# Even attention of a two-layer inference step: the value products of a head moved into one run, one head later, with TensorE held to the program's order

## Chip, cores and metric

The kernel runs on one core of one Trainium2 chip. The metric is the time of one execution on the device in microseconds, the median of the runs made; lower is better.

## What is computed

The reference is one step of a two-layer backbone on 128 prompt tokens and 512 sample tokens of width 1024. The even layer has two groups of eight attention heads: multi-head latent attention (MLA, query and key of 64 + 32 columns, values of 64) and grouped-query attention (GQA, 64 columns, two key/value heads). Prompt tokens attend to the prompt; sample tokens attend to 128 cached and 512 own keys. The odd layer, not touched here, has mLSTM and differential attention. Cut to the even layer:

```python
def attend(q, k, v):                       # scale = dk ** -0.5, blocks of 128 queries
    s = jnp.einsum('bqhgd,bthd->bhgqt', qi, k).astype(jnp.float32) * scale
    p = jax.nn.softmax(s, axis=-1).astype(v.dtype)
    return jnp.einsum('bhgqt,bthd->bqhgd', p, v)
...
o_a = attend(q_a, k_a, v_a).reshape(B, S, MLA_W) * jax.nn.silu(g_a)
o_b = attend(q_bg, kb_all, vb_all).reshape(B, S, GQA_W) * jax.nn.silu(g_b)
return jnp.concatenate([o_a, o_b], axis=-1) @ w_out, new
...
m = jax.nn.silu(cvec) @ w + b              # adaLN: shift, scale, gate of a layer
```

## The kernel before

The program is written with Tile: the text makes tiles and instructions, and a scheduler, which keeps a model of the time line, puts the instructions of each engine in an order; on the chip each engine then works in that order and waits on semaphores. Line numbers below are those of the kernel before; in the changed kernel, lines from the helper `ada_load` to the loop of `attention` stand 13 higher, lines behind that loop 23.

`even_attention` (TensorE's work from 222.8 to 402.2 us) runs 16 heads, 0 to 7 MLA and 8 to 15 GQA, over the 512 sample queries. A score tile (`head_scores`, `scores`, L596) is 128 queries by 640 keys, so a head has four of them, `i` = 0 to 3. It takes six matmuls of 320 keys for MLA (three passes over high and low parts) and four for GQA, into the PSUM tag `s2`, which has two buffers. `softexp` takes the maximum on VectorE (L603, `nm`), the exponentials and their sum on ScalarE (L606, `p` and `sm`), and the reciprocal on VectorE (L609, `rs`); GpSimd multiplies (L616). `p` has ten buffers.

For each of five key tiles `k` the four probability tiles of a head are transposed on TensorE into one PSUM tile (`head_T`, L623, tag `t1`, two buffers) and copied to SBUF as `pT` (L626 on VectorE for `k` = 2, L628 on ScalarE for the others; three buffers). `head_PV` (L634) multiplies the values of that key tile with `pT` into `o`: two matmuls in the text, which the trace shows as four, each 64 columns of the array wide. At the end of a head VectorE multiplies `o` into the gated output `og` (L710, two halves).

The loop of `attention` writes, for a head `h`, transposes of tile `k`, then the value product of tile `k - 1`, with the queries of head `h + 2` (`prep`, L764 for MLA, L749 for a pair of GQA heads), side work and score tiles in between; score tiles run up to ten ahead. The side work (`side`) is adaLN columns of the odd layer for heads 0 to 7 (`ada_cols`, L177, 32 columns of the array wide; then a ScalarE copy `adap`, two transposes L184, and small VectorE operations L186 to L195), and for heads 8 to 15 partial gate rows (`ada_gate_part`, L210), the loads and splits of the output projection's weights (`op_load`, L75 to L77) and the split of `og` into high and low parts (`op_split`, L841 and L842). The prompt's own attention goes as four `prompt_quad` pieces between the heads: scores `sp` in the tag `s2` (L647), transposes `t1p` (L660), value product `op` (L668).

PSUM has eight banks, all in use: two `s2` tiles of two banks, two `t1`, one `o`, one `pr` for queries and side work. The order between all of these is the scheduler's; in the trace of before TensorE goes from scores to transposes to value products and back many times in a head.

## Time and profile before

| | before |
|---|---|
| time, median of 3 runs | 910.01 us (910.0 to 910.73) |
| profiled execution, span from first to last instruction | 905.8 us |
| busy in the span: TensorE matmul | 852.9 us (94%) |
| VectorE, ScalarE, GpSimd | 541.2, 422.6, 396.6 us |
| even attention, 222.8 to 402.2: length, TensorE busy | 179.4, 173.66 us |
| same stage: VectorE, ScalarE, GpSimd busy | 124.35, 116.65, 103.61 us |

The profile is of one execution; the median of the runs lies 4.2 us above its span. PE is TensorE's matmuls, PEld its weight loads, DVE VectorE, ACT ScalarE, POOL GpSimd, SP the queue that issues most transfers. The chain that ended last, by the profile, is TensorE for 74% of the span and VectorE for 16%.

### The profile page before, as it was taken

The numbers are of one execution on the slowest core, as the hardware profiler recorded it, in microseconds if no ns is written. First come the engines' busy times: TensorE is split into PE (matmuls) and PEld (weight loads), VectorE is DVE, ScalarE is ACT, GpSimd is POOL, SyncE is SP. The second block draws the span as 40 slices with busy tenths as digits, with TensorE's granted clock in tenths as the row PEclk, the third lists the DMA queues.
The fourth block names the chain that finished last, engine by engine and source line by source line (L and its number), as shares of the span: only waits on it lengthen the run. The fifth ranks groups of instructions, "written<-read, shape, count | busy, mean of one in ns | idle before, by whom it ended". The sixth has DMA issues, their size and how long they took to land.

```text
span 905.8 us, 14374 instructions
## 1 busy us (share of the span) xinstructions
PE 852.9 (94%) x5418; PEld 707.2 (78%) x5418; DVE 541.2 (60%) x1125; ACT 422.6 (47%) x928; POOL 396.6 (44%) x302
## 2 busy tenths in 40 slices
PE   6999899979999999999999999999999899999997
PEld 2778788879776766668887889889989688778786
DVE  3773831993866877641386735077774736666765
ACT  5354523311655677752263324266554656443422
POOL 0144424751754646725535333422221946354930
PEclk9999999999999999999999999999999999999999
DMA  9821222220221222324412212222123122142503
GB/s 347 330 65 35 88 87 71 70 71 24 94 94 53 84 98 93 119 77 176 152 47 105 86 71 94 81 70 71 47 93 129 58 88 63 55 164 75 163 1 117
DMA packets 29641, 88.52 MB, mean 98 GB/s; under 512 B 3752, under 2 KB 6880, under 8 KB 29572
## 3 DMA queue, kind: packets, MB, share of 16 engines
q1 hardware_dynamic: 25904, 83.64, 26.4%
q10 hardware_dynamic: 3668, 3.96, 1.3%
q8 instruction: 43, 0.70, 0.3%
q14 instruction: 26, 0.21, 0.1%
HBM read 80.90 MB, written 6.68 MB: 97 GB/s over the span
## 4 chain that ended last, share of the span: by engine, by line
PE 74%; DVE 16%; issue 3%; ACT 3%; POOL 2%; DMA 1%; SPq 0%; POOLq 0%; ACTq 0%; DVEq 0%
PE acc L84 11%; PE acc L85 11%; PE acc L83 11%; PE s L596 7%; PE acc L1060 6%; PE o L634 5%; PE t L623 5%; PE acc L120 3%; PE o L1146 2%; PE pv L1460 2%; PE ada L177 1%; POOL wlo L77 1%; DVE nm L603 1%; PE gps L210 1%; PE acc L544 1%
## 5 line engine op out<-in xcount | busy, mean ns | idle before, releaser
L77 POOL TENSOR_TENSOR wlo<-raw,whi 128x1024 fp32r<-128x1024 f32 (+4 forms) x79 | 185.8, 2357 | 229.8 <-ACT whi L76 222.7
L85 PE MATMUL acc<-whi,Hl 128*128 128x512 f32 (+2 forms) x400 | 148.5, 373 | 1.6 <-DVE Hl L958 1.6
L84 PE MATMUL acc<-wlo,Hh 128*128 128x512 f32 (+2 forms) x400 | 149.2, 373 | 0.2 <-POOL wlo L77 0.2
L83 PE MATMUL acc<-whi,Hh 128*128 128x512 f32 (+2 forms) x400 | 138.9, 374 | 1.0 <-ACT qk L1064 1.0
L76 ACT CAST whi<-raw 128x1024 fp32r<-128x1024 f32 (+4 forms) x71 | 71.6, 1010 | 131.2 <-PE acc L85 80.5
L603 DVE TENSOR_REDUCE nm<-s 128x1 f32<-128x640 f32 (+1 forms) x104 | 80.9, 780 | 57.1 <-PE s L596 56.0
L616 POOL TENSOR_TENSOR p<-p,rs 128x640 f32<-128x640 f32 x64 | 79.7, 1256 | 64.2 <-DVE rs L609 62.6
L606 ACT ACTIVATE p<-s,nm 128x640 f32<-128x640 f32 (+1 forms) x104 | 79.4, 764 | 59.8 <-DVE nm L603 53.9
L85 PEld LDWEIGHTS acc<-whi,Hl 128*128 128x128 f32 x400 | 75.3, 188 | 14.7 <-DVE Hl L958 1.8
L83 PEld LDWEIGHTS acc<-whi,Hh 128*128 128x128 f32 x400 | 75.1, 188 | 14.0 <-ACT qk L1064 1.2
L84 PEld LDWEIGHTS acc<-wlo,Hh 128*128 128x128 f32 x400 | 75.4, 188 | 12.9 <-POOL wlo L77 0.6
L48 POOL TENSOR_TENSOR rs_r<-rs_h,mhalf 128x1 f32<-128x1 f32 (+4 forms) x39 | 35.6, 921 | 53.4 <-DVE rs_h L47 45.0
L623 PEld LDWEIGHTS t<-cst,p 128*128 128x128 f32 x320 | 34.6, 140 | 23.6 <-issue 22.1
L623 PE MATMUL t<-cst,p 128*128 128x128 f32 x320 | 51.3, 283 | 0.2 <-POOL p L616 0.2
L84 PE MATMUL acc<-wlo,oh 128*128 128x512 f32 (+1 forms) x124 | 48.1, 388 | 0.1
L85 PE MATMUL acc<-whi,ol 128*128 128x512 f32 (+1 forms) x124 | 47.8, 386 | 0.0
L83 PE MATMUL acc<-whi,oh 128*128 128x512 f32 (+1 forms) x124 | 46.7, 389 | 0.0
L628 ACT COPY pT<-t 128x512 f32<-128x512 f32 x64 | 37.1, 584 | 17.4 <-PE t L623 17.0
L120 PE MATMUL acc<-Hh,whi 128*128 128x320 f32 x128 | 31.3, 316 | 6.9 <-DVE og L129 6.9
L63 DVE TENSOR_REDUCE ssq<-sq 128x2 f32<-128x128 f32 (+3 forms) x19 | 11.5, 604 | 40.6 <-ACT sq L61 40.4
L885 ACT ACTIVATE junk<-xt 128x512 bf16<-128x512 f32 (+1 forms) x21 | 12.8, 610 | 49.0 <-DVE xt L883 37.7
L1060 PE MATMUL acc<-Hh,whi 128*128 128x320 f32 x128 | 32.5, 323 | 0.5 <-ACT v L1037 0.5
(380 smaller groups left out, 1983.2 us busy)
## 6 DMA issues: line engine op xcount, KB each, us to landing
adaw<-in_eada_ss_dram SPq DMA_DIRECT2D x16, 512.0 KB, 10.3
raw<-in_oada_ss_dram SPq DMA_DIRECT2D x16, 512.0 KB, 4.3
raw<-in_e_wG_dram SPq DMA_DIRECT2D x8, 512.0 KB, 3.3
raw<-in_eada_g_dram SPq DMA_DIRECT2D x8, 512.0 KB
raw<-in_e_wO_dram SPq DMA_DIRECT2D x8, 512.0 KB, 4.2
raw<-in_oada_g_dram SPq DMA_DIRECT2D x8, 512.0 KB, 3.5
raw<-in_o_wO_dram SPq DMA_DIRECT2D x8, 512.0 KB, 3.9
xT<-in_xT_dram SPq DMA_DIRECT2D x8, 320.0 KB, 5.8
```

The lines of the kernel that those rows point to most:

```text
L76: (cp or nc.scalar.copy)(hi[:, 0:m], raw[:, 0:m])
L77: nc.gpsimd.tensor_tensor(out=lo[:, 0:m], in0=raw[:, 0:m], in1=hi[:, 0:m], op=ALU.subtract)
L83: mm(out, lhsT=lh, rhs=rh, start=first, stop=False)
L84: mm(out, lhsT=lh, rhs=rl, start=False, stop=False)
L85: self.mark = mm(out, lhsT=ll, rhs=rh, start=False, stop=last)
L120: mm(acc[j][:, 0:320], lhsT=a[:, k], rhs=b[:, k, j * 320:j * 320 + 320], start=f, stop=l)
L596: self.mark = self.nc.tensor.matmul(out[:, j, 0:w], lhsT=q[0:rows, qcols], rhs=k[0:rows, a:a + w], start=i == 0, stop=i == len(passes) - 1)
L603: nc.vector.tensor_reduce(out=nm, in_=s, axis=AX.XY, op=ALU.max, negate=True)
L606: nc.scalar.activation(out=p[:, 0:n].rearrange("p (a b) -> p a b", a=s.shape[1]), in_=s, func=AF.Exp, bias=nm, accum_out=sm)
L616: self.nc.gpsimd.tensor_tensor(out=p, in0=p, in1=rs.to_broadcast([128, 640]), op=ALU.mult)
L623: self.nc.tensor.transpose(tp[:, i * 128:i * 128 + 128], p[i][:, k * 128:k * 128 + 128], self.ident)
L1060: nc.tensor.matmul(acc[j][:, 0:320], lhsT=a[:, k], rhs=b[:, k, j * 320:j * 320 + 320], start=f, stop=l)
```

## The change

Value products (`head_PV`) leave the loop over key tiles. A new inner function `values(h, pt)` issues all five of a head in one run and then the gating products; it is called in the next head, after that head's second transposition (`k` = 1), and once more at the end. `pT` therefore has seven buffers instead of three, and `p` eight instead of ten. The loop has five steps instead of six, the prompt stages come at `k` = 3 and 4 instead of 3 and 5, and the side work of heads 0 to 7 is one adaLN tile each, its second half (`rest`) one step later, where before head 0 had two and head 5 none. And a new context manager `pe_order` gives every TensorE instruction of the stage a dependency on the one before it in the text, so that the scheduler can no longer reorder TensorE there; the other engines' order is still the scheduler's.

```diff
+    @contextmanager
+    def pe_order(self):
+        ins = lambda: self.nc.cur_bb.bb.instructions
+        first = ins()[-1]
+        yield
+        now = list(ins())
+        at = next(k for k in reversed(range(len(now))) if now[k] is first) + 1
+        pe = [i for i in now[at:] if i.engine == self.mark.ins.engine]
+        for a, b in zip(pe, pe[1:]):
+            self.tc.add_manual_dep(b, a.name, mybir.DependencyInfo(mybir.DependencyClass.NoSync,
+                                                                   mybir.DependencyReason.DATA), reason="pe_order")
...
-        p, rs = self.softexp(T, s, 640, 10)
+        p, rs = self.softexp(T, s, 640, 8)
...
-        pT = T.tile([128, 512], F32, tag="pT", name="pT", bufs=3)
+        pT = T.tile([128, 512], F32, tag="pT", name="pT", bufs=7)
...
-        for h in range(nh):
+        def values(h, pt):
             o = ps.tile([128, 512], F32, tag="o", name="o", bufs=1)
-            pt = {}
-            p = [tiles.pop((h, i)) for i in range(4)]
-            for k in range(6):
-                if k < 5:
-                    pt[k] = self.head_T(T, ps, p, k)
-                if k:
-                    self.head_PV(o, V[h], cols[h], pt.pop(k - 1), k - 1)
-                if k == 0 and h + 2 < nh:
-                    prep(h + 2, P)
-                if k == 2:
-                    side(h)
-                if k in (3, 5):
-                    next(stages, None)
-                more_scores(4 * h + 5 + 1 + min(k, 3) + (1 if k >= 4 else 0))
+            for k in range(5):
+                self.head_PV(o, V[h], cols[h], pt[k], k)
             r = slice(64 * (h % 2), 64 * (h % 2) + 64)
             for j in range(2):
                 g = self.og[r, h // 2, 128 + 256 * j:384 + 256 * j]
                 nc.vector.tensor_tensor(out=g, in0=o[64 * j:64 * j + 64, 0:256], in1=g, op=ALU.mult)
+        last = None
+        for h in range(nh):
+            pt = []
+            p = [tiles.pop((h, i)) for i in range(4)]
+            for k in range(5):
+                pt.append(self.head_T(T, ps, p, k))
+                if k == 0 and h + 2 < nh:
+                    prep(h + 2, P)
+                if k == 1 and last:
+                    values(*last)
+                if k == 2:
+                    rest = side(h)
+                if k == 3 and rest:
+                    rest()
+                if k in (3, 4):
+                    next(stages, None)
+                more_scores(4 * h + 5 + 1 + min(k, 3) + (1 if k >= 4 else 0))
+            last = h, pt
+        values(*last)
...
             if h < 8:
-                for i in ((0, 1), (2,), (3,), (4,), (5,), (), (6,), (7,))[h]:
-                    self.ada_cols("o", i, ps, "pr", 1)
-                return
+                return self.ada_cols("o", h, ps, "pr", 1, split=True)
...
-        self.attention(T, ps, P, prep, [Va] * 8 + [Vb] * 8, [64 * h for h in range(8)] + [64 * (h // 4) for h in range(8)],
-                       side, quads)
+        with self.pe_order():
+            self.attention(T, ps, P, prep, [Va] * 8 + [Vb] * 8, [64 * h for h in range(8)] + [64 * (h // 4) for h in range(8)],
+                           side, quads)
```

The rest of the diff takes comments out. How the order moves shows at three places. In the rows, `s` is a score tile, `t` a transposition, `o` a value product (two matmuls in the program for each key tile, so a run of a head is x10), `gps` a gate product; the number behind a name tells tiles apart.

TensorE in a GQA head, before:

```order
L596 MATMUL s_3743<-Kb,q 128x320 x4
L634 MATMUL o<-pT,Vb 64x256 x2
L623 MATMUL t_3696<-cst,p 128x128 x4
L596 MATMUL s_3765<-Kb,q 128x320 x4
L634 MATMUL o<-pT,Vb 64x256 x2
L623 MATMUL t_3734<-cst,p 128x128 x4
L634 MATMUL o<-pT,Vb 64x256 x2
L623 MATMUL t_3756<-cst,p 128x128 x4
L596 MATMUL s_3810<-Kb,q 128x320 x4
```

and TensorE in a GQA head now, from the last step of one value run to the next:

```order
L609 MATMUL s_3680<-Kb,q 128x320 x4
L636 MATMUL t_3693<-cst,p 128x128 x4
L223 MATMUL gps<-raw,sc 32x128 x8
L609 MATMUL s_3716<-Kb,q 128x320 x4
L636 MATMUL t_3729<-cst,p 128x128 x4
L609 MATMUL s_3736<-Kb,q 128x320 x4
L636 MATMUL t_3749<-cst,p 128x128 x4
L609 MATMUL s_3756<-Kb,q 128x320 x4
L636 MATMUL t_3769<-cst,p 128x128 x4
L772 MATMUL qtp<-cst,qb 128x128 x4
L636 MATMUL t_3787<-cst,p 128x128 x4
L647 MATMUL o<-pT,Vb 64x256 x10
```

Where a value product stood between most transposes, there is now one run behind the second transposition of a head, and score tiles and transposes alternate. In the text of the sections that follow, V is such a run; T0 to T4 are the transposes of a head's five key tiles; s6 and s7 are the two score tiles behind V (here 3680 and 3716), which complete the next head, and s8 and s9 the two after them (3736 and 3756), the first of the head after that. T0 of the next head is here 3769.

TensorE in an MLA head with prompt scores (`sp`) now, from the score tile s7 on:

```order
L609 MATMUL s_2499<-Ka_1593,ql 128x320 x2
L636 MATMUL t_2514<-cst,p 128x128 x4
L197 MATMUL ada<-cst,adap 128x128 x2
L800 MATMUL qtp<-cst,qa 128x128 x4
L609 MATMUL s_2542<-Ka_1595,qh 128x320 x2
L609 MATMUL s_2542<-Ka_1596,qh 128x320 x2
L609 MATMUL s_2542<-Ka_1595,ql 128x320 x2
L636 MATMUL t_2557<-cst,p 128x128 x4
L660 MATMUL sp<-kp_1597,qp 128x128
L660 MATMUL sp<-kp_1598,qp 128x128
L660 MATMUL sp<-kp_1597,qp 128x128 x2
```

The prompt scores of a quad stand together between T4 and s9; before, the scheduler had put other score matmuls among them.

VectorE in head 8, where the first half of `og` is split, before:

```order
L710 TENSOR_TENSOR og<-o,og 64x256 x2
L842 TENSOR_TENSOR ol_3718<-og,oh_3717 128x512
L626 COPY pT<-t_3579 128x512
L609 RECIPROCAL rs<-sm 128x1
L603 TENSOR_REDUCE nm<-s_3648 128x1
L842 TENSOR_TENSOR ol_3845<-og,oh_3844 128x512
L842 TENSOR_TENSOR ol_3962<-og,oh_3961 128x512
L603 TENSOR_REDUCE nm<-s_3683 128x1
L842 TENSOR_TENSOR ol_4083<-og,oh_4082 128x512
L842 TENSOR_TENSOR ol_4206<-og,oh_4205 128x512
L609 RECIPROCAL rs<-sm 128x1
```

and now:

```order
L713 TENSOR_TENSOR og<-o,og 64x256 x2
L616 TENSOR_REDUCE nm<-s_3563 128x1
L864 TENSOR_TENSOR ol_3713<-og,oh_3712 128x512
L639 COPY pT<-t_3576 128x512
L864 TENSOR_TENSOR ol_3840<-og,oh_3839 128x512
L864 TENSOR_TENSOR ol_3957<-og,oh_3956 128x512
L616 TENSOR_REDUCE nm<-s_3599 128x1
L864 TENSOR_TENSOR ol_4078<-og,oh_4077 128x512
L864 TENSOR_TENSOR ol_4201<-og,oh_4200 128x512
L622 RECIPROCAL rs<-sm 128x1
```

The five subtractions stand among the maxima of the score tiles s6 and s7 (3563 and 3599) nearly as before; the reciprocal behind them is now that of s6.

## Rows read from the trace of the kernel before

**Rows 1.** Stretches: length, busy us (instructions) by engine, granted clock, DMA share, GB/s.
```profile
core 0: us, PE busy (x) PEld busy (x) DVE busy (x) ACT busy (x) POOL busy (x), PEclk, DMA share, GB/s
222.80:402.20 179.40, 173.66 (x1384) 118.82 (x1383) 124.35 (x261) 116.65 (x272) 103.61 (x80) 1.00 0.26 90
232.00:236.00 4.00, 2.89 (x27) 1.54 (x25) 3.23 (x6) 2.36 (x11) 3.92 (x5) 1.00 0.52 168
896.00:906.00 10.00, 3.06 (x26) 2.85 (x25) 3.73 (x11) 2.36 (x6) 1.10 (x2) 0.86 0.28 105
```

**Rows 2.** Timeline of TensorE: start us, busy us, line, output and inputs, count.
```profile
266.28 1.07 PE L177 MATMUL ada<-raw,sc 128*32 128x256 f32 x16
267.28 0.85 PE L596 MATMUL s<-Ka,qh 96*128 96x320 f32 x4
...
332.19 0.64 PE L210 MATMUL gps<-raw,sc 128*32 128x128 f32 x16
332.76 0.85 PE L596 MATMUL s<-Kb,q 128*128 128x320 f32 x4
...
357.92 0.66 PE L623 MATMUL t<-cst,p 128*128 128x128 f32 x4
358.50 0.65 PE L634 MATMUL o<-pT,Vb 128*64 128x256 f32 x4
359.09 0.66 PE L623 MATMUL t<-cst,p 128*128 128x128 f32 x4
...
363.45 0.83 PE L596 MATMUL s<-Kb,q 128*128 128x320 f32 x4
364.12 0.60 PE L623 MATMUL t<-cst,p 128*128 128x128 f32 x4
...
392.38 1.08 PE L634 MATMUL o<-pT,Vb 128*64 128x256 f32 x8
393.39 0.66 PE L623 MATMUL t<-cst,p 128*128 128x128 f32 x4
```

**Rows 3.** Timeline of score tiles through the engines (the last column: idle before).
```profile
234.07 1.30 POOL L616 TENSOR_TENSOR p<-p,rs 128x640 f32<-128x640 f32 x1
...
356.55 0.85 PE L596 MATMUL s<-Kb,q 128*128 128x320 f32 x4
357.44 0.82 DVE L603 TENSOR_REDUCE nm<-s 128x1 f32<-128x640 f32 x1 [0.67 <-PE s L596]
358.36 0.80 ACT L606 ACTIVATE p<-s,nm 128x640 f32<-128x640 f32 x1 [0.59 <-DVE rs L609]
359.35 0.16 DVE L609 RECIPROCAL rs<-sm 128x1 f32<-128x1 f32 x1 [1.01 <-ACT p L606]
359.55 2.47 POOL L616 TENSOR_TENSOR p<-p,rs 128x640 f32<-128x640 f32 x2
```

**Rows 4.** Groups of the stage: line, engine, operation, count, busy us, mean ns, idle before.
```profile
L710 DVE TENSOR_TENSOR og<-o,og 64x256 f32<-64x256 f32 x31 | 13.0, 418 | 8.8 <-PE o L634 8.4
L626 DVE COPY pT<-t 128x512 f32<-128x512 f32 x16 | 10.9, 684 | 0.7 <-PE t L623 0.4
L842 DVE TENSOR_TENSOR ol<-og,oh 128x512 fp32r<-128x512 f32 x5 | 6.3, 1292 | 0.0
L193 DVE TENSOR_SCALAR adat<-adar,cols 128x2 f32<-128x2 f32 x8 | 4.9, 614 | 0.0
L190 DVE TENSOR_SCALAR So<-adar,cols 128x2 f32<-128x2 f32 x8 | 3.5, 441 | 0.2
L760 DVE CAST Ka<-kn 64x640 fp32r<-64x640 f32 x6 | 3.1, 519 | 0.1
L315 DVE TENSOR_TENSOR qp<-qtp,qp 128x512 fp32r<-128x512 f32 x2 | 1.4, 692 | 2.1 <-ACT qp L314 2.1
L628 ACT COPY pT<-t 128x512 f32<-128x512 f32 x64 | 37.1, 584 | 17.4 <-PE t L623 17.0
L841 ACT CAST oh<-og 128x512 fp32r<-128x512 f32 x6 | 3.4, 626 | 0.0
```

More of the change, by code (lines that the diff above doesn't have):

```diff
@@ L1 @@
 import math
-from contextlib import ExitStack
+from contextlib import ExitStack, contextmanager
 import numpy as np
@@ L660, in prompt_quad @@
             nc.tensor.transpose(tp[:, j * 128:j * 128 + 128], p[:, j], self.ident)
-        pT = T.tile([128, 512], F32, tag="pT", name="pTp", bufs=3)
+        pT = T.tile([128, 512], F32, tag="pT", name="pTp", bufs=7)
         nc.vector.tensor_copy(pT, tp)
```

## Prediction, made before the changed kernel ran

> **What bounds the kernel now.** I read the stretch table first. The even attention fills 179.4 us of the 905.8 us span, from the first scores at 222.8 to the first product of the output projection at 402.2, and TensorE is busy for 173.66 of them: 5.7 us idle, with VectorE, ScalarE and GpSimd all far below it [rows 1]. So today TensorE sets the time of this stage, and whatever the stage gains or loses is passed on: the linear work behind it waits for its last product.
>
> Next I read TensorE's own timeline, start to start. Four transposes after a value product and before another take 0.58 us, four value matmuls between transposes 0.59 (358.50 to 359.09), but eight value matmuls 1.01 (392.38 to 393.39): four more cost 0.43, so about 0.15 us is paid each time TensorE goes from 128-column work (scores s, transposes t) to 64-column work (o) or back. Between s and t nothing of that kind shows: four score matmuls take 0.67 up to the transposes of 364.12, which is 4 times 0.147 and little else [rows 2]. The gate products (32 columns) pay the same price on both sides.
>
> Third, the chain of one score tile. A GQA tile whose scores start at 356.55 has its maximum at 357.44, its exponentials at 358.36, its sum's reciprocal at 359.35 and its GpSimd normalisation at 359.55; two of those take 2.47, so one is 1.25 and ends at 360.80 [rows 3]. From the start of the scores to the first moment at which a transpose can read the tile is 4.3 us with nothing in the way. For MLA heads (six score matmuls, not four) it is 4.6.
>
> **What is saved.** The order of before has 181 changes between 128-, 64- and 32-column work in this stage, that of after 69, with the same matmuls. 112 changes at 0.15 us are 16.8 us. If TensorE stayed as full as now, the stage would take 179.4 - 16.8 = 162.6 us. TensorE's own work becomes 173.7 - 16.8 = 156.9 us.
>
> The Trainium skill, "TensorEngine Tiling (Array Packing)", section Key Properties, says that changing the tiling mode drains TensorE; the 0.15 us is what that costs here, and by that rule alone the change could only win. It says nothing on what fills the time instead, which is the rest of this sum.
>
> **What is lost.** The new order is fixed, and it leaves TensorE little to do where before a value product stood ready. The last transpose of T0 (the first key tile of the next head) needs all four normalised tiles. The youngest of them, s7, is scored in the head before; between the two stand only T3, a score tile, T4 and a score tile. Value products no longer help: the whole run V comes behind T0 and T1. The tile's chain therefore closes a loop, V, s6, T2, s7, chain of s7, T0, T1, V, and its length, not TensorE's work, is a head's period. I walked the loop with the rows' durations and each engine's order of after, time 0 where V ends:
>
> GQA head with a gate product: s6 at 0, T2 0.66, gate 1.19 (0.57 [rows 2]), s7 1.76. VectorE first does two gating products (0.42 each [rows 4]), then the maximum of s6, the copy of T2 (0.68), and the maximum of s7 at 2.66. ScalarE has the copies of the gate product and of T3 (0.58) first, so s7's exponentials run 3.76 to 4.56, its sum to 4.75; normalisation 5.0 to 6.25. TensorE was ready for T0 at about 5.3 (s9 has to wait for s7's PSUM buffer, 4.65). T0's last transpose goes at 6.34; then T1, 0.5 to V, and V: 5 x 0.43 + 0.15 = 2.3. Period 9.3 us, 9.74 where a query transpose stands between. TensorE's work in it is 7.75: **1.55 us idle** in each of heads 9 to 13, 7.8 in all.
>
> MLA head with prompt transposes and prompt value product (2, 4, 6): s7 at 2.48 (adaLN product 1.0 [rows 2]), its maximum 3.66 to 4.48. On VectorE the key cast (0.52), the prompt copy (0.68) and two small adaLN operations (0.44, 0.61) stand ahead of s7's reciprocal, which comes at 7.0; T0's end at 8.57, work until V 11.2 in a period of 12.0: **0.8** each, 2.4. MLA head with prompt scores (1, 3, 5): these wait for the prompt query's low part (0.69 on VectorE, behind the adaLN operations) until 7.65, and since they take a PSUM buffer of the score pair, s9 waits for the exponentials of s8 until 9.4. Work 11.7, period 14.1: **2.4** each, 7.2. Head 7: 2.6.
>
> Head 8 carries the splitting of the output projection's first half: five casts on ScalarE (0.63 each) and five subtractions on VectorE (1.29 each [rows 4]) come between its score tiles; the maximum of s7 has three of the five ahead of it and s6's reciprocal all. Before has nearly the same VectorE order and TensorE lost one wait of 1.6 us to it, with value products to fill the rest; the bounds are 1.6 and 6.3, and I take 6.3 plus the usual 1.55, **7.9**, since the run V has gone already. Head 14 has two gate products and a weight split ahead of its last tile: **3.7**; the tail of head 15: 0.6.
>
> Start. Until the fourth tile of head 0 is normalised, TensorE has four score tiles, a query transpose, the prompt scores and three transposes: 5.6 us of work. In before that tile is done at 235.4 [rows 3]; TensorE meanwhile did a score tile and an adaLN product of later, and it was busy for 2.89 of 4 us from 232 [rows 1]. From 222.8 to 234.9 that leaves 6.4 idle; head 0, without any V, leaves 3.1 (score tiles two apart wait for each other's PSUM). Together **9.5**.
>
> Sum of idle: 9.5 + 2.4 + 7.2 + 2.6 + 7.8 + 7.9 + 3.7 + 0.6 = 41.7 us. The stage: 156.9 + 41.7 = 198.6, against 179.4: **19.2 us more**. The profiled execution ends 19.2 later, at a span of 925.0; the median of the runs stands 4.2 us above the span, and 910.0 + 19.2 = 929.2.
>
> At nothing I cost: two probability buffers fewer (the exponentials of s8 now wait for T4, which by the walk is done before ScalarE gets to them); the adaLN products spread evenly over heads 0 to 7; the gate row, which comes 20 us nearer to the end of the stage (its way through DRAM is covered by the first half of the output projection, some 14 us of products that need no gate); one weight load moved ahead of the gate row on SP. If that cover failed it would cost a few us at the projection's first evacuation.
>
> **The rivals.** (a) TensorE stays as full as before and keeps the 16.8 us: 893. For it: 97% busy today. Against it: the period of the loop is above the work in every kind of head. (b) The other side: the same loop with half the idle, because the orders of VectorE and ScalarE collide less than in my walk. The sign turns where the idle of the stage falls under 179.4 - 156.9 = 22.5 us, about 1.4 us a head. Without any collisions a GQA head's period is 8.9 (V 2.3, T0 to V 0.6, s7 at 1.76 + 4.3), so 1.1 idle, an MLA head's is near its work; with the start that is 15 to 28 us idle, and 902 to 916, middle 908. Against it: in before the chains from scores to a normalised tile are often longer than 4.3, the casts and subtractions of head 8 are real, and VectorE's rows stand in a fixed order. (c) More than I count, over 55 us idle: 943 and above; each collision delays the next head too.
>
> (d) A lower clock. The granted clock is 1.00 over the stage, also from 232 to 236; at the end of the kernel, with TensorE busy for 3.06 of 10 us, it is 0.86 [rows 1]. A fall to the lower level in head 8's stall would double up to one head's 7.75 us of work, a part of it idle anyway: about 935. The longest stall I expect is some 6 us in pieces, so it is unlikely.
>
> The Trainium skill, "TensorE: Matmul & The Clock Gate", section Why this matters for your kernels, warns of idle gaps between bursts of matmuls in mid-kernel, after which the clock drops to half; by that rule, (d) is what to look for.
>
> **How the numbers follow.** Forecast (idle 30 to 55 us, 918 to 943): 0.72; (b) 0.14; (a), with all that ends under 902: 0.05; (c) 0.05; (d) 0.04. A measurement of this kernel can tell about 0.2%, 1.8 us, from no change. Faster by more: (a) and two thirds of (b), 0.14. Within 0.2%: 0.05. Slower: 0.81. For 8 in 10 the range leaves out (a) and the lower part of (b), and most of (c): 904 to 945.
>
> **What would show it.** Right: in the stage's table TensorE's busy time near 157 of 199 us; idle just before the transposes, released by GpSimd's normalisation, 1 to 2 us in nearly every head, and a stall of several us at head 8 released by VectorE; value runs of 2.3 us; GQA periods of 9.3 to 9.7. Wrong: transposes that follow scores with no wait, or value runs that take 2.9 (no saving). The linear stages should keep their lengths. Should normalised tiles be ready within 2.6 us of GQA scores, the loop is no bound and (a) holds.

## The result, and the profile after

The changed kernel takes 933.12 us, the median of four runs (930.64 to 935.39), against 910.0 us for the kernel before: a ratio of 1.0256, 95% interval [1.0221, 1.0291]. The profiled execution is the one of 935.39 us, with a span of 933.6.

The stretch table of the changed kernel comes first (length, then busy us and instructions of TensorE, its weight loads, VectorE, ScalarE and GpSimd, then granted clock, DMA share, GB/s). The first row is the stage, from its first score to the first product of the output projection.

```profile
225.07:427.21 202.14, 174.05 (x1383) 132.79 (x1381) 122.06 (x260) 114.80 (x272) 103.66 (x80) 0.94 0.22 74
...
232.00:240.00 8.00, 7.19 (x31) 6.20 (x30) 4.51 (x9) 3.40 (x13) 5.57 (x6) 0.50 0.01 2
344.00:346.00 2.00, 1.00 (x8) 0.76 (x7) 2.00 (x4) 1.98 (x6) 0.00 (x0) 1.00 0.69 236
346.00:348.00 2.00, 1.03 (x9) 0.79 (x7) 2.00 (x4) 1.10 (x4) 0.00 (x0) 1.00 0.07 27
348.00:350.00 2.00, 1.32 (x7) 0.88 (x7) 1.69 (x6) 1.34 (x4) 1.70 (x2) 0.95 0.00 0
350.00:352.00 2.00, 1.18 (x5) 0.93 (x5) 0.31 (x2) 1.26 (x3) 2.00 (x3) 0.50 0.00 0
352.00:356.00 4.00, 4.00 (x21) 2.20 (x20) 0.00 (x0) 0.58 (x1) 1.19 (x1) 0.50 0.00 0
356.00:358.00 2.00, 2.00 (x20) 1.28 (x20) 1.30 (x3) 0.00 (x0) 0.00 (x0) 0.84 0.00 0
414.00:416.00 2.00, 0.00 (x0) 0.00 (x0) 0.00 (x0) 0.00 (x0) 2.00 (x2) 0.67 0.20 25
416.00:418.00 2.00, 1.89 (x9) 1.37 (x11) 0.00 (x0) 1.05 (x2) 0.06 (x1) 0.50 0.64 238
```

By the same two edges the stage of before is 179.12 us, with 173.38 busy, in place of the 179.40 of [rows 1], whose edges are a little wider:

```profile
222.96:402.08 179.12, 173.38 (x1383) 118.54 (x1381) 124.34 (x260) 116.65 (x272) 103.61 (x80) 1.00 0.26 90
```

The stage grew by 23.0 us, which is the whole of the difference between the medians (23.1). This one execution is another 4.8 us longer outside the stage. Ahead of it, 2.1 us go with a clock of 0.87 from 200 to 225, where before had 0.93. Behind it, 2.7 us go with two falls of the clock, to 0.50 from 746 to 749 and to a mean of 0.54 from 824 to 827, where the execution of before keeps 1.00 until 902. Two of the four runs, with spans of 928.9 and 929.1, are shorter by about as much as the whole 4.8.

Inside the stage TensorE is idle for 202.14 - 174.05 = 28.1 us, where it was 5.7. And its clock, 1.00 over the stage before [rows 1], is at 0.50, the lower of the two levels (1.2 instead of 2.4 GHz), in three places: at the start of the stage (232 to 240) and at 350 to 356 and 416 to 420. So TensorE's busy time, 174.05 us against 173.38, shows no saving, though the changes of width went from 181 to 69.

The groups of TensorE and one of VectorE in this stage (line, engine, operation, count, busy us, mean ns, idle time of the engine just before them and what ended it):

```profile
L636 PE MATMUL t<-cst,p 128*128 128x128 f32 x320 | 51.5, 281 | 12.1 <-POOL p L629 11.6 <-ACT pT L641 0.4
L609 PE MATMUL s<-Kb,q 128*128 128x320 f32 x128 | 27.4, 336 | 4.9 <-ACT p L619 4.9
L647 PE MATMUL o<-pT,Vb 128*64 128x256 f32 x160 | 23.2, 446 | 0.0
...
L864 DVE TENSOR_TENSOR ol<-og,oh 128x512 fp32r<-128x512 f32 x5 | 3.3, 683 | 0.0
```

The transposes' group of before:

```profile
L623 PE MATMUL t<-cst,p 128*128 128x128 f32 x320 | 51.3, 283 | 0.2 <-POOL p L616 0.2
```

The transposes waited 0.2 us for normalised probabilities before; now it is 11.6 us for GpSimd's normalisation. That is one wait of 5.04 us, in head 15, and twelve of 0.36 to 0.88 us. The value products wait for nothing. The timeline shows how it looks where the clock is up (head 9 to 10) and where it isn't (the ends of heads 8 and 14):

```profile
361.89 0.49 PE L636 MATMUL t<-cst,p 128*128 128x128 f32 x3
362.85 0.33 PE L636 MATMUL t<-cst,p 128*128 128x128 f32 x1 [0.48 <-POOL p L629]
363.02 0.60 PE L772 MATMUL qtp<-cst,qb 128*128 128x128 f32 x4
363.45 0.60 PE L636 MATMUL t<-cst,p 128*128 128x128 f32 x4
363.99 2.38 PE L647 MATMUL o<-pT,Vb 128*64 128x256 f32 x20
```

```profile
345.65 0.85 PE L609 MATMUL s<-Kb,q 128*128 128x320 f32 x4 [0.99 <-ACT p L619]
347.92 0.86 PE L609 MATMUL s<-Kb,q 128*128 128x320 f32 x4 [0.97 <-ACT p L619]
350.82 1.33 PE L636 MATMUL t<-cst,p 128*128 128x128 f32 x5 [0.88 <-POOL p L629]
352.07 4.54 PE L647 MATMUL o<-pT,Vb 128*64 128x256 f32 x20
416.11 1.33 PE L636 MATMUL t<-cst,p 128*128 128x128 f32 x5 [5.04 <-POOL p L629]
417.37 4.39 PE L647 MATMUL o<-pT,Vb 128*64 128x256 f32 x20
```

In the first, three of T0's four transposes go at once; the fourth waits for the tile that GpSimd finished last. A run V takes 2.3 us from start to start at full clock, and 4.3 to 4.5 behind the waits of head 8 and of head 14. The 5.04 us ahead of head 15 is one chain: a weight load that lands late, its cast on ScalarE (1.04 us) ahead of the last tile's exponentials, its subtraction on GpSimd (2.34) ahead of that tile's normalisation.

```profile
411.38 1.04 ACT L76 CAST whi<-raw 128x1024 fp32r<-128x1024 f32 x1 [0.98 <-DMA raw<-in_e_wO_dram]
412.51 2.34 POOL L77 TENSOR_TENSOR wlo<-raw,whi 128x1024 fp32r<-128x1024 f32 x1 [3.26 <-ACT whi L76]
```

### The profile page after: what moved, and what is told of

Its sections match the earlier page's. It is cut to its first block, busy times and chain, and to the rows that moved or that the text cites. A ratio compares the mean times of both kernels' runs of the same rounds, so it can differ in the third digit from the quotient of the medians.

```text
span 933.6 us, 14383 instructions
## 1 busy us (share of the span) xinstructions
PE 858.1 (92%) x5418; PEld 725.3 (78%) x5418; DVE 538.3 (58%) x1125; ACT 420.8 (45%) x928; POOL 396.2 (42%) x302
## 4 chain that ended last, share of the span: by engine, by line
PE 67%; DVE 17%; POOL 4%; issue 4%; ACT 4%; DMA 2%; SPq 0%; POOLq 0%; ACTq 0%; DVEq 0%
PE acc L84 11%; PE acc L85 11%; PE acc L83 11%; PE acc L1082 6%; PE s L609 5%; PE o L647 4%; PE acc L120 3%; POOL p L629 2%; PE t L636 2%; DVE nm L616 2%; PE pv L1482 2%; PE o L1168 2%; PE ada L190 1%; POOL wlo L77 1%; PE acc L557 1%
## 5 line engine op out<-in xcount | busy, mean ns | idle before, releaser
L85 PEld LDWEIGHTS acc<-whi,Hl 128*128 128x128 f32 x400 | 75.6, 189 | 14.8 <-DVE Hl L980 1.8
L83 PEld LDWEIGHTS acc<-whi,Hh 128*128 128x128 f32 x400 | 75.5, 189 | 14.1 <-ACT qk L1086 1.2
L636 PE MATMUL t<-cst,p 128*128 128x128 f32 x320 | 51.5, 281 | 12.1 <-POOL p L629 11.6
L636 PEld LDWEIGHTS t<-cst,p 128*128 128x128 f32 x320 | 40.0, 144 | 17.3 <-POOL p L629 15.2
L120 PE MATMUL acc<-Hh,whi 128*128 128x320 f32 x128 | 31.5, 318 | 6.9 <-DVE og L129 6.9
L622 DVE RECIPROCAL rs<-sm 128x1 f32<-128x1 f32 x104 | 16.6, 160 | 35.8 <-ACT p L619 33.1
```

Of the source, the lines that this page charges most:

```text
L83: mm(out, lhsT=lh, rhs=rh, start=first, stop=False)
L85: self.mark = mm(out, lhsT=ll, rhs=rh, start=False, stop=last)
L120: mm(acc[j][:, 0:320], lhsT=a[:, k], rhs=b[:, k, j * 320:j * 320 + 320], start=f, stop=l)
L636: self.nc.tensor.transpose(tp[:, i * 128:i * 128 + 128], p[i][:, k * 128:k * 128 + 128], self.ident)
```

## The experiments

Every run is compared with the kernel before on the same chip. The stage column uses the two edges above; "changes" are the changes of matmul width in TensorE's order.

| run | changes | median us | ratio, 95% interval | stage | idle in it |
|---|---|---|---|---|---|
| before | 181 | 910 | 1 | 179.1 | 5.7 |
| the change | 69 | 933.12 | 1.0256 [1.0221, 1.0291] | 202.1 | 28.1 |
| e1_order_only | 171 | 948.28 | 1.0437 [1.0408, 1.0465] | 217.1 | 28.2 |
| e2_runs_only | 178 | 912.66 | 1.0041 [1.0025, 1.0057] | 179.6 | 5.3 |
| e3_run_first | 69 | 925.32 | 1.0191 [1.0158, 1.0224] | 193.1 | 23.1 |
| e4_no_norm | 69 | 919.31 | 1.0111 [1.0091, 1.0131] | 187.7 | 18.5 |
| e5_ahead | 69 | 918.99 | 1.0076 [1.0050, 1.0101] | 186.5 | 18.5 |
| e6_runs_free | 86 | 920.13 | 1.0112 [1.0081, 1.0144] | 188.7 | 19.9 |
| e9_spread | 69 | 930.83 | 1.0217 [1.0169, 1.0264] | 199.2 | 27.9 |
| e11_fill | 69 | 930.97 | 1.0215 [1.0167, 1.0263] | 197.1 | 21.5, with the filling counted as busy |
| e12_sched_order | 71 | 911.01 | 1.0012 [0.9995, 1.0030] | 176.8 | 15.0 |
| e13_sched_ahead | 73 | 913.41 | 1.0040 [1.0024, 1.0056] | 180.2 | 16.7 |
| e14_three_mends | 69 | 924.44 | 1.0160 [1.0131, 1.0188] | 189.2 | 23.6 |
| e15_half_runs | 104 | 913.23 | 1.0040 [1.0017, 1.0064] | 181.1 | 14.5 |

### The two halves of the change apart

e1_order_only puts the fixed order alone on the kernel before:

```
-        self.attention(T, ps, P, prep, ...)
+        with self.pe_order():
+            self.attention(T, ps, P, prep, ...)
```

> The kernel before with one thing added: TensorE is held to the program's order over the attention. Value products stay between the transposes (171 changes of column width, 181 before), so nothing is saved. Loop theory: from s7 to the next head's T0 there are now two value products and more, about 4.7 us of work against a chain of 4.5, so the transposes wait little (under 0.5 us a head); what is left of the loss is what any fixed order loses here: the start, the prompt scores of heads 1, 3 and 5, head 8, the last heads, about 25 to 33 us of idle in all. Stage 195 to 205 us, time 925 to 935. Rival, that the place of the run V alone makes the loss: stage within 5 us of before, 910 to 915.

e2_runs_only is the changed kernel without it: the runs are written whole, and the scheduler is free to take them apart.

> The changed kernel without the fixed order: values are still written a head late and in one run, but the scheduler is free on TensorE and breaks the runs up again (178 changes of column width in its order). Loop theory: neither the saving nor the stalls, so about the time of before, 906 to 914. Rival, that the buffers (eight p, seven pT) or the spread adaLN work cost by themselves: 918 or more.

The stage's row in e1:

```profile
225.26:442.34 217.08, 188.86 (x1383) 129.55 (x1381) 118.95 (x260) 116.14 (x272) 104.16 (x80) 0.93 0.21 69
```

The order alone loses 38.0 us in the stage, more than either theory gave it: 22.5 us of idle time and 15.5 us of busy time, at a mean clock of 0.93. e2 has 178 changes and is about the kernel before again, 0.4% slower: without the fixed order the runs hardly exist, and the other buffers and the spread adaLN work cost little. So the saving exists only under the fixed order: the order costs 38.0, the rest of the change under it gives 217.08 - 202.14 = 14.9 back, and 23.0 is left.

The two fixed orders are idle for nearly the same time, 28.2 and 28.1 us, but not in the same places. In e1 the value products wait for their own transposed copies, and the adaLN products for theirs (4.0 us):

```profile
L647 PE MATMUL o<-pT,Vb 128*64 128x256 f32 x160 | 27.5, 424 | 7.8 <-ACT pT L641 7.6
```

In this order a product often stands right behind what it needs; the run, a head late, removed these waits and made the one ahead of T0. That the two sums are equal is chance: they are made of different waits.

### What the transposes wait for

Three runs act on the loop that the prediction named (V, s6, T2, s7, the chain of s7, T0, T1, V). e3_run_first puts V ahead of T0:

```
+            if last:
+                values(*last)
             for k in range(5):
                 pt.append(self.head_T(T, ps, p, k))
...
-                if k == 1 and last:
-                    values(*last)
```

> The changed kernel with the run V moved ahead of T0 (it stood behind T1); order and 69 changes of width as in the changed kernel. Loop theory: V now fills the gap between s9 and T0 in which the normalisation of s7 was waited for; from s7 to T0 there is 5.0 us of GQA work against a chain of 4.5. Idle before transposes, released by GpSimd, goes from about 1 us a head to near nothing in GQA heads and heads 2, 4, 6; the waits at the prompt scores of heads 1, 3, 5 and most of the start stay. 910 to 917, 14 to 20 us below the changed kernel. Rival, that the loss is the fixed order's whatever stands in the gap: 925 to 933.

e4_no_norm leaves out the multiplication on GpSimd that normalises the sample heads' probabilities:

```
-        self.nc.gpsimd.tensor_tensor(out=p, in0=p, in1=rs.to_broadcast([128, 640]), op=ALU.mult)
```

> The changed kernel without the normalisation of the sample heads' probabilities on GpSimd (the multiplication by the reciprocal is left out, so the chain of a tile is 1.5 us shorter; TensorE does the same work). Loop theory: each GQA head loses its 1.5 us, heads 2, 4, 6 some 0.8, the start and head 14 one to three: 912 to 919. Heads 1, 3, 5 keep their waits at the prompt scores. Rival, that TensorE waits for PSUM or ScalarE first: less than 5 us gained, 926 or more.

e5_ahead issues each score tile one place earlier, with one more probability buffer and one transposed buffer fewer:

```
-                more_scores(4 * h + 5 + 1 + min(k, 3) + (1 if k >= 4 else 0))
+                more_scores(4 * h + 5 + 2 + min(k, 3) + (1 if k >= 4 else 0))
```

> The changed kernel with every score tile issued one place earlier in the written order (nine probability buffers instead of eight, six transposed ones instead of seven): the first tile behind each run of value products is then not the one that the next head's first transpose needs, and the normalisation on GpSimd has about 1.8 us more. Theory (a fixed order makes TensorE wait at the first transpose of each head for a normalisation that started too late): those waits go in the heads that run full otherwise, 1.5 us each in heads 9 to 13 and part of heads 1 to 7, so the stage is 10 to 15 us shorter than the changed kernel's 202.1, 917 to 924 us in all. Rival (the engine that normalises, or ScalarE in front of it, can't go faster than it does, so an earlier score only waits longer for its buffer): within 3 us of the changed kernel, 929 to 936.

The transposes' group in e3 and in e5:

```profile
L636 PE MATMUL t<-cst,p 128*128 128x128 f32 x320 | 50.8, 287 | 0.8 <-POOL p L629 0.4 <-ACT pT L641 0.2
```

```profile
L636 PE MATMUL t<-cst,p 128*128 128x128 f32 x320 | 48.3, 277 | 0.9 <-POOL p L629 0.5 <-ACT pT L641 0.3
```

All three shorten the stage, by 9.0, 14.5 and 15.6 us, and in e3 and e5 the wait for GpSimd falls from 11.6 to 0.4 and 0.5. So the loop was the cause of these waits, and its length, not GpSimd's rate, set them: e5 keeps every normalisation and gains as much as e4, which has none. Not all of the gain is idle time: 4.1, 4.9 and 6.0 us of it are busy time of TensorE. Much of that is the value products of the GQA heads, 23.2 us in the changed kernel, where the clock fell behind two waits, 19.0 in e3 and e5 and 20.7 in e4. e5's time came as its theory said (919.0 in 917 to 924), e4's just above the upper end of its theory (919.3, 912 to 919). e3 came at the rival's end (925 to 933), since it met a wait that I hadn't seen. TensorE's gate product in head 10, with VectorE's row ahead of it:

```profile
367.69 0.69 DVE L777 TENSOR_TENSOR q<-qtp,q 64x512 fp32r<-64x512 f32 x1
368.49 0.65 PE L223 MATMUL gps<-raw,sc 128*32 128x128 f32 x16 [2.20 <-issue]
```

The profile names no releaser ("issue"). But query transposes and gate products share the one PSUM buffer "pr", and the product starts 0.1 us after VectorE's second read of the query transposes is done. So I take it that it waits for that buffer; no run gave the product a buffer of its own. With V no longer between them, nothing covers that read. In head 8 the same wait is 5.51 us, since the five splitting subtractions stand ahead of the read.

### The stall of head 8, and the clock

e9_spread holds the five casts and subtractions back to heads 9 to 13, one in each:

```
                 if 9 <= h < 14:
-                    self.op_split(self.R, 0, h - 9)
+                    with self.tc.issue_after(self.amark.ins), self.tc.issue_after(self.dmark.ins):
+                        self.op_split(self.R, 0, h - 9)
```

> The changed kernel, with the five subtractions on VectorE that split the gated output, and the casts on ScalarE before them, held back so that one of each stands in each of heads 9 to 13, instead of all five in head 8. Theory (the burst holds back the maxima of head 8's scores, TensorE waits about 4 us there, and its clock falls after it): head 8 to head 9 takes 9.3 to 10 us instead of 12.7, and the run of value products behind it 2.3 instead of 4.5: 4 to 6.5 us less, 926.5 to 929. Rival (the burst lies in time that VectorE had to spare, the wait comes from the first query product of the new heads): 931.5 to 935.

e11_fill gives TensorE useless products to do in the two places:

```
+            self.fill(ps, {(9, 0, 2): 2, (9, 0, 3): 3, (15, 0, 3): 18}.get((self.h, k, i), 0))
             self.nc.tensor.transpose(tp[:, i * 128:i * 128 + 128], p[i][:, k * 128:k * 128 + 128], self.ident)
...
+                self.fill(ps, 3 if h == 8 and k >= 3 else 0)
                 more_scores(4 * h + 5 + 1 + min(k, 3) + (1 if k >= 4 else 0))
```

> The changed kernel with products of no use (128x512, into a free buffer) in the places where TensorE waits longest: 11 of them in head 8's four waits ahead of head 9, and 18 in the 5 us ahead of the first transpose of head 15. They take only time in which TensorE waited. Theory (the clock at 0.50 behind these two waits is their after-effect: it falls because TensorE stood): both runs of value products take 2.3 us instead of 4.4, and their neighbours gain as well: 4 to 6 us less, 927 to 929.5. Rival (the clock falls there for another reason): within 1.5 us of the changed kernel, 931.5 to 935, or more by what the products push back.

The end of head 8 and, behind the dots, that of head 14, in e9 and then in e11:

```profile
348.41 2.38 PE L647 MATMUL o<-pT,Vb 128*64 128x256 f32 x20
...
413.48 4.53 PE L647 MATMUL o<-pT,Vb 128*64 128x256 f32 x20
```

```profile
350.48 0.76 PE L637 MATMUL t<-cst,p 128*128 128x128 f32 x5 [0.18 <-POOL p L629]
351.18 2.38 PE L654 MATMUL o<-pT,Vb 128*64 128x256 f32 x20
...
413.20 0.76 PE L637 MATMUL t<-cst,p 128*128 128x128 f32 x5 [1.08 <-POOL p L629]
413.89 2.38 PE L654 MATMUL o<-pT,Vb 128*64 128x256 f32 x20
```

In e9 head 8 takes 9.8 us to the next T0 instead of 12.7 and its run 2.38 instead of 4.54, so the burst was the cause of that stall, and the clock fell because of the stall. The next score tile starts 5.8 us earlier than in the changed kernel, that of head 14 only 3.0 us earlier: each of heads 9 to 13 has a subtraction more now. The idle time of the stage is what it was (27.9 against 28.1); its 2.9 us less are busy time. Head 14's stall stays. In e11 the transposes come when they came before (350.48 against 350.82), so the filling took only time in which TensorE waited; both runs take 2.38, and the stage is 5.1 us shorter, as expected. The medians (930.83 and 930.97) lie about 2 us under the changed kernel's, with intervals that overlap widely. Both lie between the two ranges on record, above the theory's (926.5 to 929 and 927 to 929.5) and under the rival's (931.5 to 935): the traces show the mechanism, the runs alone would not prove a gain. The Trainium skill, "TensorE: Matmul & The Clock Gate", section Why this matters for your kernels, warns that the clock drops to half behind idle gaps between bursts of matmuls. The trace agrees ahead of head 15, where TensorE stood for 5.04 us; in head 8 the clock fell with no wait longer than 1.0 us, so there the measurement goes further than the warning.

The third place, the start, no run mended. It goes with the written order: from 230 to 240 the mean clock is 0.50 to 0.71 in the changed kernel and in e1, e3, e4, e5, e9, e11 and e14, and 1.00 in before, e2, e6, e12, e13 and e15, where the scheduler chose the order, or most of it.

### Is it the written order, or any?

e6_runs_free fixes TensorE only against the runs: what is written between two runs stays between them, in any order.

```
-        for a, b in zip(pe, pe[1:]):
-            self.tc.add_manual_dep(b, a.name, ...)
+        run, seg = None, []
+        for i in pe:
+            if i.name in self.vrun:
+                for a in (seg if seg else [run] if run else []):
+                    dep(i, a)
+                run, seg = i, []
+            else:
+                if run is not None:
+                    dep(i, run)
+                seg.append(i)
```

> Each head's ten value products stay one run, a head late, but TensorE's order is fixed only against these runs: what is written between two runs stays between them, and there the scheduler chooses the order. Theory (the fixed order within a head costs the idle time, the runs themselves gain): the 0.15 us per change of width stay gained (some 85 changes against 181 of before, 14 us), and half or more of the 28 us of idle time of the changed kernel goes, 898 to 914 us. Rival (the run itself, with what may not cross it, is what makes TensorE wait, since all five copies must be there at once): idle time as in the changed kernel, 926 to 936.

It came between the two: 188.7 us, with 9.6 of 19.9 us idle still ahead of transposes that wait for GpSimd. So I let the scheduler place whole runs among everything else and fixed the order that came out (ORDER lists ranges of TensorE's instructions as written, V a run of ten):

```
+ORDER = """0:12 24:28 12:24 44:48 40:41 60:61 28:40 41:42 61:62 48:54 74:82 42:43 ...
...
+        for x in ORDER.split():
+            if x == "V":
+                pe, runs = pe + runs[:10], runs[10:]
+            else:
+                a, b = map(int, x.split(":"))
+                pe += rest[a:b]
         for a, b in zip(pe, pe[1:]):
```

> The runs of ten value products stay whole and TensorE's order stays fixed over the stage, as in the changed kernel; but the order is not the written one: it is the one that the scheduler chooses when nothing else is fixed than that a run isn't broken (71 changes of width against 181 of before). Theory (what the change loses is the written order; neither a fixed order nor whole runs cost anything): the 110 changes that are gone at 0.15 us are 16.5 us, and the idle time stays near that of before, within some 6 us: stage 163 to 172 against 179, 894 to 904 us. Rival (a whole run holds TensorE back by itself, since it needs five copies at once and the next head's work behind it comes later): 910 to 921, as with runs that nothing may cross.

e13_sched_ahead is the same with the edit of e5 and the order that the scheduler chose for it.

> As e12_sched_order, with score tiles written one place earlier (nine probability buffers, six transposed ones) and the scheduler's order for that program. Theory (score tiles further ahead give GpSimd's normalisation room): up to 4 us less than e12_sched_order, 890 to 903. Rival (in an order that the scheduler chose the waits for it are gone already, and one transposed buffer less costs something): 0 to 5 us more than e12_sched_order.

The stage and the groups that wait in e12:

```profile
223.49:400.26 176.77, 161.76 (x1382) 124.59 (x1380) 120.37 (x260) 114.84 (x272) 103.40 (x80) 1.00 0.27 91
```

```profile
L656 PE MATMUL t<-cst,p 128*128 128x128 f32 x320 | 49.6, 279 | 7.2 <-ACT pT L661 3.5 <-DVE pT L659 2.3 <-DVE rs L642 0.9
L629 PE MATMUL s<-Kb,q 128*128 128x320 f32 x128 | 26.6, 332 | 2.6 <-ACT p L639 2.4
```

Half of my theory held: a fixed order with whole runs needn't lose anything, 911.0 us is no different from before. The other half fell: nothing is won, and the time lies in the rival's range (910 to 921), not in the theory's (894 to 904). The rival's reason isn't borne out either: a run of value products waits for nothing here. TensorE has 11.6 us less to do (161.76 against 173.38, both at a clock of 1.00) and 9.3 us more of waiting. The waits are new ones: transposes for the copies that empty their two PSUM buffers, scores for the exponentials that empty theirs. At the end of the stage, where only transposes and runs are left:

```profile
388.94 0.66 PE L656 MATMUL t<-cst,p 128*128 128x128 f32 x4 [0.62 <-ACT pT L661]
390.20 1.09 PE L656 MATMUL t<-cst,p 128*128 128x128 f32 x8 [0.61 <-ACT pT L661]
```

A copy takes 0.58 us, four transposes 0.43, so TensorE outruns the copies; in before, value products stood between most transposes. That the mixture hid the difference is my inference, and e15 tests it. e13 is 2.4 us slower than e12, as its rival had it.

The stage of e12 is 2.3 us shorter than that of before, and yet the time isn't. In the profiled execution 0.5 us of it goes ahead of the stage and 2.9 behind it, where the clock is at 0.50 twice (481 to 483 and 798 to 801).

e15_half_runs was to restore that mixture, with a run of six products for key tiles 0 to 2 ahead of the head's last transposes and one of four in the next head, again in the scheduler's order:

```
+                if k == 4:
+                    values(h, pt, range(0, 3))
                 pt.append(self.head_T(T, ps, p, k))
```

> Each head's value products in two runs, six products for key tiles 0 to 2 ahead of the head's last transpose and four for tiles 3 and 4 in the next head, in the order that the scheduler chooses around them (104 changes of width against 181 of before and 71 of e12_sched_order), fixed as a chain. Theory (a run of ten leaves stretches of transposes and scores alone, which outrun two buffers and the engines that empty them; shorter runs keep the mixture of before): 77 changes fewer are 11.5 us, and idle time rises by 5 us or less: 899 to 906. Rival (the supply of probabilities sets the stage's pace however TensorE is ordered, so what TensorE saves comes back as waits): 908 to 914, as with e12_sched_order.

```profile
L658 PE MATMUL t<-cst,p 128*128 128x128 f32 x319 | 52.1, 280 | 6.7 <-ACT pT L663 5.0 <-DVE rs L644 1.0 <-DVE pT L661 0.6
```

Its rival came true: 14.5 us idle, with nearly the same waits as e12. So runs of ten are not what brings most of them.

### The mends together

e14_three_mends joins the edits of e3, e5 and e9 in the written order.

> The written order again, with three of its waits mended at once: the run ahead of the first transpose of the next head instead of behind it, score tiles one place earlier, the five splits spread over heads 9 to 13. Theory (the waits found so far make up most of the loss, and they are in different places): of the 202.1 us of the stage 9 go with the run's place, 4 to 8 with the earlier tiles, 4 to 6 with the splits and the clock behind them, so 179 to 186, 906 to 915 us. Rival (each mend takes the same wait, which is there only once): no better than the best of them alone, 917 to 921.

Neither came true: 189.2 us is worse than e5 alone (186.5).

```profile
L223 PE MATMUL gps<-raw,sc 128*32 128x128 f32 x128 | 5.2, 278 | 5.5 <-issue 4.5 <-ACT gp L225 1.0
```

No transpose waits for GpSimd, but the gate products pay what e3 found (4.5 us, in e5 nothing of the kind), and the scores wait for the exponentials nearly as long as in e5 (7.1 us, 8.2 in e5). In this fixed order the next wait stood close behind the one that was mended.

No version beats the kernel before. The best of them, e12, can't be told from it.

## Why the prediction was right

By sign and range it was right: 929.2 was forecast, 904 to 945; 933.1 came. The stage grew by 23.0 us instead of 19.2. The forecast case was met by its time (918 to 943) and missed by its condition: it wanted 30 to 55 us idle, and 28.1 came, the upper end of what rival (b) had (15 to 28). The time got there all the same, since TensorE was busy for 174 us and not for 156.9. So the direction and the loop were foreseen, and that the size came so near is luck. Point by point:

**The loop.** It held. Heads 11 and 13 (a gate product, no query transposes) take 9.29 us from T0 to T0, forecast 9.3; heads 10 and 12, with query transposes, 10.3 and 10.1 (9.74); the MLA heads with prompt products 11.6 to 11.9 (12.0), those with prompt scores 14.2, 14.3 and 13.1 (14.1). e3, e4 and e5 each cut the loop at another place, and the waits went. But the sign that I named, 1 to 2 us ahead of the transposes in nearly every head, was not there: twelve of these waits are 0.36 to 0.88 us.

**The saving, 16.8 us.** Too large: it is about 12. e12 and before, both at full clock, differ by 11.6 us of TensorE's busy time for 110 changes, 0.106 each instead of 0.15. e1 and the changed kernel differ by 14.8 us of busy time for 102 changes, but e1's clock is lower (0.93 against 0.94). I had read 0.15 from transposes and value products next to each other [rows 2] and taken it for every change. Behind a score tile it is less. In the trace of before:

```profile
388.84 0.82 PE L596 MATMUL s<-Kb,q 128*128 128x320 f32 x4
389.60 0.65 PE L634 MATMUL o<-pT,Vb 128*64 128x256 f32 x4
```

Four score matmuls take 0.76 us up to value products and 0.67 up to transposes (363.45 to 364.12 in [rows 2]): the change of width costs 0.09 there.

**The idle time, 41.7 us.** 28.1 came. Three things make most of the difference: the work in a loop, the start, and head 8, which has its own point below. The work in a loop is larger than I had it (a GQA head is busy for 8.36 of its 9.29 us, not 7.75), so the same period holds less idle time. The rows are those of head 11 and of the start until T0 of head 1:

```profile
225.07:236.90 11.83, 9.44 (x45) 7.87 (x43) 7.05 (x15) 4.79 (x11) 6.13 (x5) 0.72 0.01 1
236.90:251.31 14.41, 12.80 (x93) 10.96 (x91) 10.15 (x22) 8.34 (x23) 9.30 (x9) 0.87 0.23 73
...
373.15:382.44 9.29, 8.36 (x73) 6.35 (x73) 5.21 (x13) 6.30 (x14) 7.30 (x5) 1.00 0.36 116
```

And the start, 9.5 in my sum, has only 4.0 us idle; the rest of that time TensorE works at a lower clock (0.72 and 0.87). My test, a busy time "near 157 of 199 us", failed for these reasons and the saving: it is 174 of 202.

**Rival (d), the clock, chance 0.04.** This is the step that failed: the sum has the lower clock at nothing. The clock fell in head 8's stall, as (d) said, and in two places that (d) did not name. A mean of 0.94 over 202.1 us is at most 12.1 us at stake (TensorE stood for a part of that time), and 174.05 less those is 161.9, about what e12 needs at full clock. The reason that I gave against it, that the longest stall would be "some 6 us in pieces", was no reason: the stall did come in pieces, TensorE was still busy for 1.0 to 1.3 of each 2 us from 344 to 350, and from 350 the clock was at 0.50.

So the sum came near by three errors: saving 5 too large, idle time 14 too large, clock 12 left out.

**Head 8, 7.9 us.** Too large: 3.5 us idle in the 12.7 us from T0 to T0. I had taken 1.29 us for each subtraction from [rows 4]; in the changed kernel they take 0.68. The run behind it at half clock took most of that back: the next head lasted 12.0 us instead of 9.3.

**Head 14, 3.7 us.** Too small: 6.6 us, 5.04 of them in one wait ahead of T0 and 1.18 ahead of the second gate product. I had the gate products and the split, but not that the weights for the split would land late and hold back ScalarE's cast, with the last tile's exponentials behind it.

**The price from which it turns.** "Where the idle of the stage falls under 22.5 us" the sign should change; e4, e5 and e6, with 18.5 to 19.9 us idle, are still slower than before, since 156.9 was too low for the work. With 162 the point is 17 us, and e12 at 15.0 lies just under it: its stage is 2.3 us shorter, which its time doesn't show.

**What stays open.** Why the clock falls at the start in the written order, and what it alone costs there, since no run mended that place. And why TensorE's 11.6 us of saved work come back as waits even in the scheduler's order. No other engine is full in e12 (VectorE 120, ScalarE 115 of 177 us). Two PSUM buffers for transposes and two for scores fit the waits that are named, but no run with more of them was made.

## What to carry to other kernels

A change that makes the busiest engine's work cheaper by fixing its order must be costed by the longest loop through the other engines, from its own output back to its own input; here, at 97% busy, the scheduler's interleaving was worth more than the 12 us of changes that the runs saved. When one wait is mended in a fixed order, run it before adding the mends up: here three mends worth 9, 15.6 and 3 us together gave 13. And where a change adds waits of a few us, put the lower clock behind them into the sum.

## What the runs showed of the hardware

The clock fell without a long idle stretch: it was at 1.00 until 348, 0.95 to 350 and 0.50 from there, and no single wait ahead of that was longer than 1.0 us. It rose again between 356 and 358, when TensorE had been busy throughout since 352.

A subtraction on VectorE with both inputs in SBUF (128x512) costs 0.68 us when GpSimd rests, as in the changed kernel's five, and more when it starts behind a GpSimd instruction. Before, the five stood beside GpSimd's work; two of them, and GpSimd's instruction:

```profile
340.41 3.45 DVE L842 TENSOR_TENSOR ol<-og,oh 128x512 fp32r<-128x512 f32 x2
340.95 2.36 POOL L77 TENSOR_TENSOR wlo<-raw,whi 128x1024 fp32r<-128x1024 f32 x1 [2.34 <-ACT whi L76]
```

The pair lasts until 343.86, 0.55 us past GpSimd's end at 343.31. e9, which spreads the subtractions, shows it one by one, and both ways round:

```profile
354.25 0.69 DVE L865 TENSOR_TENSOR ol<-og,oh 128x512 fp32r<-128x512 f32 x1
354.39 1.67 POOL L629 TENSOR_TENSOR p<-p,rs 128x640 f32<-128x640 f32 x1 [4.05 <-DVE rs L622]
...
365.27 1.25 POOL L629 TENSOR_TENSOR p<-p,rs 128x640 f32<-128x640 f32 x1 [2.99 <-DVE rs L622]
365.29 1.78 DVE L865 TENSOR_TENSOR ol<-og,oh 128x512 fp32r<-128x512 f32 x1
```

Where the subtraction starts first, it takes its 0.69 us and GpSimd's normalisation 1.67 instead of 1.25; where GpSimd starts first, by 0.02 us, it takes its 1.25 and the subtraction 1.78. The Trainium skill, "SBUF — State Buffer", section Summary: rules for kernel authors, says that of a VectorE instruction with two SBUF inputs and a GpSimd instruction that reads SBUF the one that issues second is blocked until the first is done. The rows agree. So my mean of 1.29 us from [rows 4] held the neighbour's time, and was not the price of the subtraction.
